# An output projection by seven products: four of them accumulate in one pair of banks, two operands are loaded in place, and part of the sums goes to GpSimd

## The chip, the cores and the metric

The kernel runs on one core of a Trainium2 chip. The time is that of the device in microseconds (us) for one execution. The engines of a core are TensorE (PE, matrix products; PEld is its loading of weights), VectorE (DVE), ScalarE (ACT), GpSimd (POOL) and SyncE (SP), which issues all DMA transfers of this kernel from one queue. Operands lie in SBUF, products in eight PSUM banks of 128 x 512 float32.

## The reference

One layer with four groups of mixers, each 512 wide, over 1024 tokens. Only the last line is touched by the change: the four mixers' outputs, side by side 1024 x 2048, are multiplied by a 2048 x 2048 matrix and added to x, all in float32.

```python
h = rms_norm(x, norm_g[l]) @ w_in[l]
...
y_a = gmlp_mixer(a_u, a_v, a_v_gain[l], a_ws[l], a_bs[l]) * jax.nn.silu(a_z)
y_b = dsa_mixer(...) * jax.nn.silu(b_z)
y_c = mla_mixer(...) * jax.nn.silu(c_z)
y_d = band_mixer(...) * jax.nn.silu(d_z)
x = x + jnp.concatenate([y_a, y_b, y_c, y_d], axis=-1) @ w_out[l]
```

## The kernel before

Most of the program computes the input projections and the four mixers; each mixer leaves its output y transposed (feature rows, token columns) in DRAM as `y_d`. The last input projection, that of A's gate, ends at about 1594 us, and the output projection takes the rest.

The output projection is done in two halves. The first takes groups B and D and adds them to x, with the result in DRAM (`pt_d`); the second takes groups C and A and adds them to that, with the result in `out`. Within a half the two token halves and the two groups form a 2 x 2 block matrix: a11 and a21 are the first group's first and last 512 tokens, a12 and a22 the second group's. The block product is made with seven products instead of eight (Strassen's method in Winograd's form): S1 to S4 are sums and differences of these blocks, and the weight blocks b are combined in the same way into t1 to t4. `prepare` makes the seven operands of a half: it loads y in tiles `ys` (128 x 1024, three buffers), forms the sums, and splits each operand into a high part `yh` (a cast on ACT) and a low part `yl` (a difference on DVE). A float32 product then takes three matmuls: high x high, high x low, low x high. The high and low parts of a half take seven of the eight large buffers that hold x and its low parts until the last input projection has read them, so each operand can be written only when a quarter of x has been read for the last time.

`out_unit` is called four times per half, for 512 output columns each; the text numbers the units 0 to 7. A unit loads four weight tiles `wo` and four residual tiles `xr` (one for each token half t and row pair jp, 128 x 2 x 512), combines the weights on DVE, splits them into `wh` (ACT) and `wl` (POOL) with three buffers each, runs the seven products and adds them to the residual tiles. A product is 48 matmuls (two halves of four 128-row steps, four blocks of rows) into two PSUM banks. Units 0 to 7 all use the same banks: X and Y from the four of `pp`, Z and W from the other four. DVE adds products from PSUM to `xr`; the product P1 is first copied to SBUF by ACT (`p1`), as three residual blocks need it.

The order on PE is written out by hand; that on the other engines is set by a scheduler when the program is built, in which the operands' and the weights' work has high priority and the adds to the residual have not. Each engine works through its queue in order. An instruction waits for the semaphores of what it reads and of what must have read its target before.

Of the kernel before, what the change touches and what calls it, by code (L numbers as in the profile page):

```python
# [18 lines left out]
P = 128  # L19
# [116 lines left out]
def build(tc, i, out, dbg=None):  # L136
# [1105 lines left out]
    A11, S2, S1, A12, S3, A22, S4 = range(7)  # L1242
# [6 lines left out]
    def load_y(g, kt):  # L1249
        t = op.tile([P, SEQ], F32, tag="ys", name="ys", bufs=3)  # L1250
        S.dma_start(t, y_d[512 * g + P * kt:512 * g + P * (kt + 1)])
        return t

    def prepare(g1, g2, part):
        for at in (S3, A22, S4) if part else (A11, S2, S1, A12):
            slots[at] = (big("th", "yh"), big("tl", "yl"))
        with hi_prio():
            if part == 0:
# [52 lines left out]
    def out_unit(g1, g2, c0, src, dst, rp, last):  # L1311
        cs = slice(c0, c0 + 512)
        ks1 = [load_wo(g1, h, c0) for h in range(2)]
        ks2 = [load_wo(g2, h, c0) for h in range(2)]
# [6 lines left out]
        with hi_prio():  # L1321
            ws["b11"] = [split_w(b11) for b11, _ in ks1]
# [5 lines left out]
            ws["t2"] = [split_w(t) for t in t2]  # L1328
            ws["t1"] = [split_w(b11) for b11, _ in ks1]
            ws["b21"] = [split_w(b21) for b21, _ in ks2]  # L1330
            for (_, b12), (_, b22) in zip(ks1, ks2):
                V.tensor_tensor(b12, b22, b12, op=ALU.subtract)
            ws["t3"] = [split_w(b12) for _, b12 in ks1]
            for (b21, _), t in zip(ks2, t2):
                V.tensor_tensor(b21, b21, t, op=ALU.subtract)
            ws["t4"] = [split_w(b21) for b21, _ in ks2]
            ws["b22"] = [split_w(b22) for _, b22 in ks2]
# [4 lines left out]
        def add(t, n, pss):  # L1342
            for jp in range(2):
                o = res[t, jp][:, :, 256 * n:256 * n + 256]
                V.tensor_tensor(o, o, f(pss[jp]), op=ALU.add)  # L1345
# [26 lines left out]
        for jp in range(2):  # L1372
            store(1, jp, 0, 2)
        if last:
            for jp in range(2):
                store(0, jp, 0, 1)
        add(0, 1, Z)
        for jp in range(2):
            store(0, jp, int(last), 2)

    for n, (g1, g2) in enumerate(((1, 3), (2, 0))):
        for part in range(2):
            prepare(g1, g2, part)
# [4 lines left out]
        for c in range(4):  # L1388
            out_unit(g1, g2, 512 * c, x_d if n == 0 else pt_d, pt_d if n == 0 else out, rp, n == 1 and c == 3)
# [35 lines left out]
```

## Time and profile before

| | |
|---|---|
| median of 3 runs | 1953.63 us (1952.82 to 1954.27) |
| the profiled execution | 1952.85 us |
| its span (what the trace covers) | 1951.0 us |
| PE, DVE, ACT, POOL busy | 97%, 61%, 40%, 37% |
| output projection, roughly | 1594 us to the end |

The time of the profiled execution is 1.85 us more than its span. A busy share of PE counts any time in which a matmul is under way; it does not say how fast the matmuls follow each other. The granted clock (PEclk) is a share of 2.4 GHz.

### The profile page before, as it was taken

How to read it: one execution, taken by the hardware profiler on the slowest of the kernel's cores; microseconds unless marked ns; L12 is line 12 of the kernel's file. 1: busy time of each engine (PE TensorE's matmuls, PEld its weight loads, DVE VectorE, ACT ScalarE, POOL GpSimd, SP SyncE). 2: the span in 40 equal slices, each digit the busy share in tenths (PEclk: the TensorE clock that was granted, in tenths of full speed). 3: DMA queues.
4: the chain of work that ended last, by engine and by line, in shares of the span. 5: the costliest groups of instructions: out<-in, count | busy, mean ns of one | idle time of the engine just before them, and what ended most of it. 6: DMA issues, size and time to landing. Idle time of an engine off the chain costs nothing.

```text
span 1951.0 us, 34949 instructions
## 1 busy us (share of the span) xinstructions
PE 1886.5 (97%) x13068; PEld 1755.6 (90%) x13068; DVE 1189.0 (61%) x3057; ACT 778.0 (40%) x1565; POOL 718.4 (37%) x784
## 2 busy tenths in 40 slices
PE   5999999999999999999999999999999998998999
PEld 4988998899888999999998889998888778998999
DVE  6514899887466553488836665734343568569644
ACT  6424533331455454344325555644453243223221
POOL 4121256763344443222223333422222133444543
PEclk8999999999999999999999999999999998999999
DMA  7231122223322222333334443243333756447443
GB/s 220 87 109 33 33 66 71 71 66 85 102 81 74 59 66 68 112 127 116 103 106 117 103 117 93 68 138 96 98 98 117 256 202 204 144 158 253 141 140 120
DMA packets 186269, 220.40 MB, mean 113 GB/s; under 512 B 26051, under 2 KB 136820, under 8 KB 185972
## 3 DMA queue, kind: packets, MB, share of 16 engines
q1 hardware_dynamic: 186100, 218.17, 37.0%
q8 instruction: 103, 1.69, 0.4%
q14 instruction: 66, 0.54, 0.1%
HBM read 153.35 MB, written 60.58 MB: 110 GB/s over the span
## 4 chain that ended last, share of the span: by engine, by line
PE 85%; DVE 6%; DMA 5%; SPq 1%; issue 1%; ACT 1%; POOL 1%; DVEq 0%; POOLq 0%; ACTq 0%
PE pp L206 60%; PE sc L206 14%; PE po L206 6%; PE sc L210 5%; DMA duo<-vd_d 1%; DMA ys<-y_d 1%; DMA nat<-qk_d 1%; DVE yl L243 1%; SPq L302 1%; DVE ys L1279 0%; DVE xr L1345 0%; DVE xr L1353 0%; DMA sw<-in_w_in 0%; DMA wr<-in_w_in 0%; SPq L327 0%
## 5 line engine op out<-in xcount | busy, mean ns | idle before, releaser
L420 POOL TENSOR_TENSOR wl<-wr,wh 128x512 fp32r<-128x512 f32 x192 | 255.1, 1329 | 526.4 <-ACT wh L419 470.1
L206 PE MATMUL pp<-wh,xh 128*128 128x256 f32 x1536 | 436.9, 284 | 0.0
L206 PE MATMUL pp<-wh,xl 128*128 128x256 f32 x1536 | 433.5, 282 | 0.0
L206 PE MATMUL pp<-wl,xh 128*128 128x256 f32 x1536 | 432.6, 282 | 0.0
L206 PE MATMUL pp<-xh,wh 128*128 128x512 f32 x768 | 309.2, 403 | 0.0
L206 PE MATMUL pp<-xh,wl 128*128 128x512 f32 x768 | 304.4, 396 | 0.0
L206 PE MATMUL pp<-xl,wh 128*128 128x512 f32 x768 | 304.0, 396 | 0.0
L206 PEld LDWEIGHTS pp<-wl,xh 128*128 128x128 f32 x1536 | 290.6, 189 | 1.2
L206 PEld LDWEIGHTS pp<-wh,xh 128*128 128x128 f32 x1536 | 289.8, 189 | 1.2
L206 PEld LDWEIGHTS pp<-wh,xl 128*128 128x128 f32 x1536 | 288.8, 188 | 0.0
L419 ACT CAST wh<-wr 128x512 fp32r<-128x512 f32 x192 | 118.9, 619 | 358.0 <-PE pp L206 312.9
L1292 POOL TENSOR_TENSOR wl<-wo,wh 128x512 fp32r<-128x512 f32 x96 | 138.9, 1451 | 169.4 <-ACT wh L1291 153.0
L530 POOL TENSOR_SCALAR sS<-sS,den 128x640 f32<-128x640 f32 (+7 forms) x160 | 115.9, 726 | 215.8 <-DVE den L529 156.8
L206 PEld LDWEIGHTS pp<-xh,wl 128*128 128x128 f32 x768 | 144.5, 188 | 35.0
L206 PEld LDWEIGHTS pp<-xl,wh 128*128 128x128 f32 x768 | 145.0, 189 | 28.9
L206 PEld LDWEIGHTS pp<-xh,wh 128*128 128x128 f32 x768 | 144.7, 188 | 29.2 <-issue 0.3
L528 ACT ACTIVATE sS<-sS,nm 128x640 f32<-128x640 f32 (+7 forms) x160 | 119.0, 744 | 125.3 <-DVE nm L525 111.9
L206 PE MATMUL pp<-wh,yh 128*128 128x256 f32 x512 | 147.3, 288 | 16.9 <-DVE xr L1345 13.9
L206 PE MATMUL pp<-wl,yh 128*128 128x256 f32 x512 | 146.4, 286 | 2.8 <-POOL wl L1292 2.7
L206 PE MATMUL pp<-wh,yl 128*128 128x256 f32 x512 | 146.0, 285 | 0.0
L700 DVE TENSOR_SCALAR_CACHE_REDUCE t<-score,cand 128x896 bf16<-128x896 f32 (+4 forms) x155 | 135.9, 877 | 4.2
L243 DVE TENSOR_TENSOR pl<-sc,ph 128x512 fp32r<-128x512 f32 (+1 forms) x152 | 92.2, 616 | 55.6 <-ACT ph L242 48.6
(262 smaller groups left out, 4115.2 us busy)
## 6 DMA issues: line engine op xcount, KB each, us to landing
wr<-in_w_in SPq DMA_DIRECT2D x192, 256.0 KB, 2.8
ys<-y_d SPq DMA_DIRECT2D x32, 512.0 KB, 3.8
wo<-in_w_out SPq DMA_DIRECT2D x32, 512.0 KB, 3.8
xt<-in_x SPq DMA_DIRECT2D x32, 256.0 KB, 4.7
xr<-in_x SPq DMA_DIRECT2D x16, 512.0 KB, 4.9
pt_d<-xr SPq DMA_DIRECT2D x16, 512.0 KB, 6.6
xr<-pt_d SPq DMA_DIRECT2D x16, 512.0 KB, 5.4
out<-xr SPq DMA_DIRECT2D x14, 512.0 KB, 6.9
```

Source lines behind the costliest of these rows:

```text
L206: T.matmul(o, l, r, start=start, stop=stop, skip_group_check=True)
L210: T.transpose(o, t, ident)
L243: V.tensor_tensor(lo, src, hi.bitcast(F32), op=ALU.subtract)
L302: S.dma_start(raw[:, :, o:o + n], rows[:, c0:c0 + n].rearrange("(k p) c -> p k c", p=P))
L419: A.copy(hi, raw)
L420: G.tensor_tensor(lo, raw, hi.bitcast(F32), op=ALU.subtract)
L528: A.activation(sS[:, :tot], sS[:, :tot], AF.Exp, bias=nm[:, 0:1], accum_out=den[:, 0:1])
L530: G.tensor_scalar(sS[:, :tot], sS[:, :tot], den[:, 1:2], 0.5, op0=ALU.mult, op1=ALU.mult)
L700: V.tensor_scalar(t1[:, :n], score[:, SOFF[b]:SOFF[b] + n], th, None, op0=op, op1=ALU.add, accum_out=cnt[:, b - 2:b - 1])
L1292: G.tensor_tensor(lo, src, hi.bitcast(F32), op=ALU.subtract)
```

## The change

Of the seven products, four (A11, S2, S3 and A22) now accumulate in one pair of banks, X. After each of the first three ACT copies what the bank holds (`keep`), and the copy is added to a residual block. The other three share Y. So a unit needs four banks; even units take those of `pp`, odd units the other four. The products come in another order (A11, A12, S2, S1, S3, S4, A22) and the weight combinations change their signs accordingly. Three of the adds of a copy are done by GpSimd instead of DVE.

In `prepare` the operands A11 and A12, which need no sums, are loaded straight into the tile of their low part and split there. The differences and sums for S3 and S4 move to GpSimd, with S3 kept in four tiles `s3` of its own. The weights of a half's first unit are loaded ahead of its operands.

```diff
-    A11, S2, S1, A12, S3, A22, S4 = range(7)
+    PRODUCTS = A11, A12, S2, S1, S3, S4, A22 = range(7)
...
-                for kt in range(4):
-                    q, r = load_y(g1, kt), load_y(g2, kt)
-                    a11, a21, a12, a22 = q[:, 0:512], q[:, 512:1024], r[:, 0:512], r[:, 512:1024]
-                    split_y(kt, A11, a11)
-                    V.tensor_tensor(a22, a21, a22, op=ALU.add)
-                    V.tensor_tensor(a11, a22, a11, op=ALU.subtract)
-                    split_y(kt, S2, a11)
-                    split_y(kt, S1, a22)
-                    split_y(kt, A12, a12)
-                return
-            for kt in range(4):
-                q = load_y(g1, kt)
-                V.tensor_tensor(q[:, 0:512], q[:, 0:512], q[:, 512:1024], op=ALU.subtract)
-                split_y(kt, S3, q[:, 0:512])
+            for at, k in ((A11, 0), (A12, 1)):
+                hi, lo = slots[at]
+                for kt in range(4):
+                    r0 = 512 * gs[k] + P * kt
+                    S.dma_start(lo[:, kt].bitcast(F32), y_d[r0:r0 + P, 0:512])
+                    split(hi[:, kt], lo[:, kt], lo[:, kt].bitcast(F32))
             for kt in range(4):
-                r = load_y(g2, kt)
-                a12, a22 = r[:, 0:512], r[:, 512:1024]
+                a11, a21 = load(0, kt)
+                a22 = load(1, kt)[1]
+                V.tensor_tensor(a22, a21, a22, op=ALU.add)
+                V.tensor_tensor(a11, a22, a11, op=ALU.subtract)
+                split_y(kt, S2, a11)
+                split_y(kt, S1, a22)
+            s3 = [op.tile([P, 512], F32, tag="s3", name="s3", bufs=4) for _ in range(4)]
+            for kt in range(4):
+                a11, a21 = load(0, kt)
+                G.tensor_tensor(s3[kt], a11, a21, op=ALU.subtract)
+                split_y(kt, S3, s3[kt])
+            for kt in range(4):
+                a12, a22 = load(1, kt)
+                G.tensor_tensor(a12, a12, a22, op=ALU.subtract)
+                G.tensor_tensor(a12, a12, s3[kt], op=ALU.add)
+                split_y(kt, S4, a12)
                 split_y(kt, A22, a22)
-                V.tensor_tensor(a12, a12, a22, op=ALU.subtract)
-                for t in slots[S3]:
-                    V.tensor_tensor(a12, a12, t[:, kt].bitcast(F32), op=ALU.add)
-                split_y(kt, S4, a12)
...
-        X, Y = ([pp.tile([P, 512], F32, tag="pp", name="pp", bufs=4) for _ in range(2)] for _ in range(2))
-        Z, W = [bank() for _ in range(2)], [bank(), obank()]
+        if odd:
+            X, Y = [bank() for _ in range(2)], [bank(), obank()]
+        else:
+            X, Y = ([pp.tile([P, 512], F32, tag="pp", name="pp", bufs=4) for _ in range(2)] for _ in range(2))
...
+        def keep(pss):
+            ts = [rp.tile([P, 512], F32, tag="p1", name="p1", bufs=6) for _ in range(2)]
+            for t, ps in zip(ts, pss):
+                with hi_prio():
+                    A.copy(t, ps)
+            return ts
...
-        product(X, A11, ws["b11"], True)
-        for jp in range(2):
-            p1 = rp.tile([P, 512], F32, tag="p1", name="p1", bufs=2)
-            A.copy(p1, X[jp])
-            for t, n in ((0, 1), (1, 1), (1, 0)):
-                o = res[t, jp][:, :, 256 * n:256 * n + 256]
-                V.tensor_tensor(o, o, f(p1), op=ALU.add)
-        product(Y, S2, ws["t2"], True)
+                eng.tensor_tensor(o, o, f(pss[jp]), op=ALU.add)
+
+        product(X, A11, ws[A11], True)
+        add(0, 0, keep(X), G)
+        product(Y, A12, ws[A12], True)
+        add(0, 0, Y)
+        product(X, S2, ws[S2], False)
+        add(0, 1, keep(X), G)
+        product(Y, S1, ws[S1], True)
+        z1 = keep(Y)
+        product(X, S3, ws[S3], False)
+        add(1, 1, keep(X), G)
+        add(1, 1, z1)
+        product(Y, S4, ws[S4], False)
         add(0, 1, Y)
-        product(Z, S1, ws["t1"], True)
-        add(1, 1, Z)
-        product(X, A12, ws["b21"], False)
-        add(0, 0, X)
-        product(Y, S3, ws["t3"], False)
-        add(1, 1, Y)
-        add(1, 0, Y)
-        product(W, A22, ws["t4"], True)
-        add(1, 0, W)
-        product(Z, S4, ws["b22"], False)
...
+        product(X, A22, ws[A22], False)
+        add(1, 0, X)
```

Two places in the engines' queues matter below, both in unit 0. The first is POOL's queue. Before, it holds the weights' low parts one after the other (here those of the second to fifth product, L1292):

```order
L1292 TENSOR_TENSOR wl_18528<-t2_18521,wh_18527 128x512
L1292 TENSOR_TENSOR wl_18532<-t2_18524,wh_18531 128x512
L1292 TENSOR_TENSOR wl_18536<-wo_18497,wh_18535 128x512
L1292 TENSOR_TENSOR wl_18540<-wo_18499,wh_18539 128x512
L1292 TENSOR_TENSOR wl_18544<-wo_18501,wh_18543 128x512
L1292 TENSOR_TENSOR wl_18548<-wo_18503,wh_18547 128x512
```

In the changed kernel the queue at the same place reads as follows. L1298 is a weight's low part (wl_18548 is the third product's second, wl_18552 and wl_18556 are the fourth product's), L1283 and L1284 make S4, and L1359 adds a kept product to a residual tile (xr_18513 and xr_18517 are the first token half's, p1_18639 and p1_18640 the first product).

```order
L1298 TENSOR_TENSOR wl_18548<-t2_18540,wh_18547 128x512
L1283 TENSOR_TENSOR ys_18492<-ys_18492 128x512
L1284 TENSOR_TENSOR ys_18484<-ys_18484,s3_18453 128x512
L1359 TENSOR_TENSOR xr_18513<-xr_18513,p1_18639 128x2x256
L1284 TENSOR_TENSOR ys_18492<-ys_18492,s3_18454 128x512
L1298 TENSOR_TENSOR wl_18552<-wo_18366,wh_18551 128x512
L1298 TENSOR_TENSOR wl_18556<-wo_18368,wh_18555 128x512
L1283 TENSOR_TENSOR ys_18500<-ys_18500 128x512
L1359 TENSOR_TENSOR xr_18513<-xr_18513,p1_18743 128x2x256
L1298 TENSOR_TENSOR wl_18564<-wo_18366,wh_18563 128x512
L1359 TENSOR_TENSOR xr_18517<-xr_18517,p1_18640 128x2x256
```

So operand work and adds to the residual now stand between the weights' low parts, and the first product's add to the second residual tile comes last of these rows.

The second place is DVE's queue around its first add of a product from PSUM. Before (L1345 adds from PSUM, L1353 adds the copied product, L1279 and L243 are operand work, L1335 weights):

```order
L1353 TENSOR_TENSOR xr_18505<-xr_18505,p1_18635 128x2x256
L1335 TENSOR_TENSOR wo_18501<-wo_18501,t2_18521 128x2x256
L1279 TENSOR_TENSOR ys_18474<-ys_18474,yh_18430 128x512
L1353 TENSOR_TENSOR xr_18507<-xr_18507,p1_18635 128x2x256 x2
L1335 TENSOR_TENSOR wo_18503<-wo_18503,t2_18524 128x2x256
L243 TENSOR_TENSOR yl_18435<-ys_18465,yh_18434 128x512
L1345 TENSOR_TENSOR xr_18505<-xr_18505,pp_18581 128x2x256
```

In the changed kernel (L1359 adds from PSUM here, pp_18589 and pp_18590 being the pair Y; yl_18385 and yl_18387 are S4's and A22's low parts, yl_20338 is already that of the second half's A11):

```order
L243 TENSOR_TENSOR yl_18385<-ys_18476,yh_18384 128x512
L243 TENSOR_TENSOR yl_18387<-ys_18476,yh_18386 128x512
L243 TENSOR_TENSOR yl_18387<-ys_18484,yh_18386 128x512
L243 TENSOR_TENSOR yl_18387<-ys_18492,yh_18386 128x512
L243 TENSOR_TENSOR yl_20338<-yl_20338,yh_20337 128x512
L243 TENSOR_TENSOR yl_18385<-ys_18484,yh_18384 128x512
L243 TENSOR_TENSOR yl_20338<-yl_20338,yh_20337 128x512
L1359 TENSOR_TENSOR xr_18513<-xr_18513,pp_18589 128x2x256
L243 TENSOR_TENSOR yl_20338<-yl_20338,yh_20337 128x512 x2
L243 TENSOR_TENSOR yl_18385<-ys_18492,yh_18384 128x512
L243 TENSOR_TENSOR yl_18387<-ys_18500,yh_18386 128x512
L1359 TENSOR_TENSOR xr_18517<-xr_18517,pp_18590 128x2x256
```

The adds of the copied product have left this queue; the two adds from PSUM stand between differences of operands that POOL has made before, and each reads a residual tile to which POOL adds first.

## Rows read from the trace of the kernel before

**Rows 1.** The page: the span, and busy time of each engine.

```profile
span 1951.0 us, 34949 instructions
...
PE 1886.5 (97%) x13068; PEld 1755.6 (90%) x13068; DVE 1189.0 (61%) x3057; ACT 778.0 (40%) x1565; POOL 718.4 (37%) x784
```

**Rows 2.** Waits of PE from 1580 us on: total, times, longest, in us.

```profile
PE pp L206 <- DVE xr L1345: 13.9, 3, 5.4
PE pp L206 <- POOL wl L1292: 2.7, 3, 1.5
PE sc L206 <- POOL wl L1292: 2.6, 4, 1.0
```

**Rows 3.** Busy us by stretch: PE, PEld, DVE, ACT, POOL, clock, DMA share, GB/s.

```profile
1594.00:1631.00 37.00, 25.78 (x200) 24.70 (x199) 34.65 (x46) 13.38 (x23) 17.00 (x9) 0.90 0.63 217
1689.40:1729.70 40.30, 40.30 (x338) 40.30 (x337) 22.44 (x29) 9.76 (x16) 19.21 (x14) 1.00 0.47 158
```

**Rows 4.** The chain that ended last, from 1500 us: start, length, what.

```profile
1630.85 6.74 PE pp L206 x42
...
1643.35 5.76 PE sc L206 x48
1649.11 11.52 PE pp L206 x96
...
1729.75 8.65 PE pp L206 x72
...
1807.02 7.31 PE pp L206 x42
...
1825.86 11.52 PE pp L206 x96
```

**Rows 5.** PE in order of time: last input projection, first stall on DVE's add.

```profile
1593.80 0.40 PE L206 MATMUL pp<-xh,wl 128*128 128x512 f32 x1
...
1625.54 0.55 PE L206 MATMUL pp<-wh,yh 128*128 128x256 f32 x1 [4.82 <-DVE xr L1345]
```

**Rows 6.** DVE's groups from 1594 us on, by form: adds from PSUM, from SBUF.

```profile
L1345 DVE TENSOR_TENSOR xr<-xr,pp 128x512 f32<-128x512 f32 x64 | 41.8, 682 | 37.1 <-PE pp L206 37.1
L1353 DVE TENSOR_TENSOR xr<-xr,p 128x512 f32<-128x512 f32 x48 | 40.8, 879 | 39.1 <-DMA xr<-pt_d 13.7 <-DMA xr<-in_x 12.1 <-ACT p L1350 11.1
```

**Rows 7.** DVE in order of time, 1786 to 1792 us.

```profile
1786.77 1.29 DVE L243 TENSOR_TENSOR yl<-ys,yh 128x512 fp32r<-128x512 f32 x2
1787.98 1.77 DVE L1279 TENSOR_TENSOR ys<-ys,yh 128x512 f32<-128x512 f32 x1
1789.79 1.67 DVE L1279 TENSOR_TENSOR ys<-ys,yl 128x512 f32<-128x512 f32 x1
```

**Rows 8.** POOL in order of time: two beside adds from PSUM, two beside rows 7.

```profile
1643.39 2.56 POOL L1292 TENSOR_TENSOR wl<-wo,wh 128x512 fp32r<-128x512 f32 x2 [3.56 <-DMA wo<-in_w_out]
...
1787.86 3.05 POOL L1292 TENSOR_TENSOR wl<-wo,wh 128x512 fp32r<-128x512 f32 x2 [2.33 <-ACT wh L1291]
```

**Rows 9.** ACT in order of time: casts that waited for x's second quarter.

```profile
1571.04 1.14 ACT L242 CAST yh<-ys 128x512 fp32r<-128x512 f32 x2 [2.70 <-PE pp L206]
```

**Rows 10.** ACT's groups from 1594 us on, by form.

```profile
L242 ACT CAST yh<-ys 128x512 fp32r<-128x512 f32 x39 | 23.7, 619 | 67.1 <-DVE ys L1279 24.1 <-DMA ys<-y_d 18.2 <-DVE ys L1271 14.1
...
L1350 ACT COPY p<-pp 128x512 f32<-128x512 f32 x16 | 9.2, 583 | 4.8 <-PE pp L206 4.6
```

**Rows 11.** DMA issues from 1594 us on: count, size, median us to landing.

```profile
ys<-y_d SPq DMA_DIRECT2D x20, 512.0 KB, 3.7
...
pt_d<-xr SPq DMA_DIRECT2D x16, 512.0 KB, 6.6
...
y_d<-hs SPq DMA_DIRECT2D x4, 256.0 KB, 4.8
```

**Rows 12.** DVE in unit 5: the first use of its third residual tile.

```profile
1837.04 0.69 DVE L1353 TENSOR_TENSOR xr<-xr,p 128x512 f32<-128x512 f32 x1 [2.19 <-issue]
```

More of the change, by code (lines that the diff above doesn't have):

```diff
@@ L1247, in split_y, with renew, prepare, load @@
         split(*(t[:, kt] for t in slots[at]), src)
[L1249 to L1255, printed above, removed]
-            slots[at] = (big("th", "yh"), big("tl", "yl"))
+    def renew(ats):
+        for at in ats:
+            slots[at] = (big("th", "yh"), big("tl", "yl"))
+    def prepare(gs):
+        renew(PRODUCTS)
+        def load(k, kt):
+            t = op.tile([P, SEQ], F32, tag="ys", name="ys", bufs=3)
+            S.dma_start(t, y_d[512 * gs[k] + P * kt:512 * gs[k] + P * (kt + 1)])
+            return t[:, 0:512], t[:, 512:1024]
@@ L1309, in rows_of, with out_unit @@
         return slice(512 * t + 256 * jp, 512 * t + 256 * jp + 256)
-    def out_unit(g1, g2, c0, src, dst, rp, last):
+    def out_unit(ks, c0, src, dst, rp, odd, last):
         cs = slice(c0, c0 + 512)
-        ks1 = [load_wo(g1, h, c0) for h in range(2)]
-        ks2 = [load_wo(g2, h, c0) for h in range(2)]
+        ks1, ks2 = ks
         res = {}
@@ L1321, in out_unit @@
         with hi_prio():
-            ws["b11"] = [split_w(b11) for b11, _ in ks1]
+            ws[A11] = [split_w(b11) for b11, _ in ks1]
+            ws[A12] = [split_w(b21) for b21, _ in ks2]
             t2 = []
@@ L1327, in out_unit @@
                 V.tensor_tensor(t2[-1], b22, b11, op=ALU.subtract)
-            ws["t2"] = [split_w(t) for t in t2]
-            ws["t1"] = [split_w(b11) for b11, _ in ks1]
-            ws["b21"] = [split_w(b21) for b21, _ in ks2]
+            ws[S2] = [split_w(t) for t in t2]
+            ws[S1] = [split_w(b11) for b11, _ in ks1]
             for (_, b12), (_, b22) in zip(ks1, ks2):
                 V.tensor_tensor(b12, b22, b12, op=ALU.subtract)
-            ws["t3"] = [split_w(b12) for _, b12 in ks1]
@@ L1334, in out_unit @@
             for (b21, _), t in zip(ks2, t2):
                 V.tensor_tensor(b21, b21, t, op=ALU.subtract)
-            ws["t4"] = [split_w(b21) for b21, _ in ks2]
-            ws["b22"] = [split_w(b22) for _, b22 in ks2]
-        X, Y = ([pp.tile([P, 512], F32, tag="pp", name="pp", bufs=4) for _ in range(2)] for _ in range(2))
-        Z, W = [bank() for _ in range(2)], [bank(), obank()]
-        f = lambda t: t.rearrange("p (j c) -> p j c", j=2)
-        def add(t, n, pss):
+            ws[S3] = [split_w(b12) for _, b12 in ks1]
@@ new lines, in out_unit @@
+            ws[S4] = [split_w(b22) for _, b22 in ks2]
+            ws[A22] = [split_w(b21) for b21, _ in ks2]
+        if odd:
+            X, Y = [bank() for _ in range(2)], [bank(), obank()]
+        else:
+            X, Y = ([pp.tile([P, 512], F32, tag="pp", name="pp", bufs=4) for _ in range(2)] for _ in range(2))
+        f = lambda t: t.rearrange("p (j c) -> p j c", j=2)
+        def keep(pss):
[4 more added lines that the diff above has]
+            return ts
@@ L1343, in add @@
+        def add(t, n, pss, eng=V):
             for jp in range(2):
                 o = res[t, jp][:, :, 256 * n:256 * n + 256]
-                V.tensor_tensor(o, o, f(pss[jp]), op=ALU.add)
-        product(X, A11, ws["b11"], True)
-        for jp in range(2):
-            p1 = rp.tile([P, 512], F32, tag="p1", name="p1", bufs=2)
-            A.copy(p1, X[jp])
-            for t, n in ((0, 1), (1, 1), (1, 0)):
-                o = res[t, jp][:, :, 256 * n:256 * n + 256]
-                V.tensor_tensor(o, o, f(p1), op=ALU.add)
@@ L1372, in out_unit @@
         for jp in range(2):
-            store(1, jp, 0, 2)
+            store(0, jp, 0, 2)
         if last:
             for jp in range(2):
-                store(0, jp, 0, 1)
-        add(0, 1, Z)
+                store(1, jp, 1, 2)
+        product(X, A22, ws[A22], False)
+        add(1, 0, X)
         for jp in range(2):
-            store(0, jp, int(last), 2)
+            store(1, jp, 0, 1 if last else 2)
     for n, (g1, g2) in enumerate(((1, 3), (2, 0))):
-        for part in range(2):
-            prepare(g1, g2, part)
+        load_ks = lambda c: [[load_wo(g, h, 512 * c) for h in range(2)] for g in (g1, g2)]
+        ks = load_ks(0)
+        prepare((g1, g2))
         if n == 0:
@@ L1388, in build @@
         for c in range(4):
-            out_unit(g1, g2, 512 * c, x_d if n == 0 else pt_d, pt_d if n == 0 else out, rp, n == 1 and c == 3)
+            out_unit(ks if c == 0 else load_ks(c), 512 * c, x_d if n == 0 else pt_d, pt_d if n == 0 else out, rp, c % 2, n == 1 and c == 3)
     if dbg is not None:
```

1 line of the change is left out of this document (removed).

## The prediction

> **What bounds the kernel now.** The page comes first: TensorE (PE) is busy for 97% of the span [rows 1], so a stage can gain only what PE stands idle there. The table by stages shows where that is. In a middle unit of the output projection PE is busy for all of 40.3 us, with VectorE (DVE) at 22.4 and GpSimd (POOL) at 19.2 us. From 1594 to 1631 PE works for 25.8 of 37 us, DVE for 34.7 [rows 3]. The chain gives the unit boundaries [rows 4]. A product is 48 matmuls in 5.76 us, so a unit of seven needs 40.32 us. Unit 0 runs from 1594.20, where the last input projection ends [rows 5], to 1649.11: 54.9 us, 14.6 too many. Units 3 and 4 together run from 1729.75 to 1825.86: 96.1 us instead of 80.6, 15.5 too many. The other units show no excess, so some 30 us are at stake, all where the operands of a half are being made. The table of waits names the releaser of the largest stalls: DVE's add of a product into the residual, 13.9 us [rows 2]. It stands in DVE's queue behind the sums and differences of the operands, and PE must not write that bank before it is read [rows 5].
>
> The second thing to see is why DVE is slow there. Its adds from PSUM take 682 ns whatever happens, its adds between SBUF tiles 879 ns on average [rows 6]. The timeline shows the cause: two such operations start every 0.60 us when alone, but take 1.77 and 1.67 us when two POOL operations run beside them, and those two take 3.05 us together instead of the 2.56 beside adds from PSUM [rows 7, 8]. So the SBUF operations of DVE and those of POOL exclude each other for most of their length: one of each costs 1.72 us (the mean of the two DVE rows), against 1.28 for POOL alone and 0.60 for DVE alone.
>
> **What the change does, part by part.** *Residual adds.* A unit loses 12 of its 20 DVE adds: four of the six between SBUF tiles, and eight from PSUM, which did not exclude POOL. POOL gains six, of the size of its own 1.28 us rows. In SBUF time that DVE and POOL must share, a unit goes from (6 + 8) x 0.60 + 14 x 1.28 = 26.3 us to (2 + 8) x 0.60 + 20 x 1.28 = 31.6 us. The eight are DVE's operations on weights. That fits in 40.3, so in units 1, 2, 5, 6 and 7 I cost it at nothing: a weight part has two half products, 5.76 us, between its buffer's release and its use, and the cast (0.62) and POOL's difference (1.28) take 1.9 of them. Without that cover two POOL adds in front of a part would cost up to 2.6 us.
>
> *Copies.* ScalarE makes eight copies of a product per unit instead of two, 6 x 0.58 = 3.5 us [rows 10], beside 9.8 us of work in 40.3 [rows 3]. PE may not go on in the bank until its copy is done, but always has another product of 5.76 us in between, so nothing is added. Unit 0's first copy is an exception: its tile lies where the last gate results are still being stored, and those stores land 4.8 us after issue [rows 11]; the third product would wait for it until about 1613, which is earlier than the wait found below.
>
> *Operands.* Per half DVE goes from 52 operations to 36, all between SBUF tiles, and POOL from none to 12: 52 x 0.60 = 31.2 us of shared time become 36 x 0.60 + 12 x 1.28 = 37.0. The two loaded in place need no sums, and eight loads of 256 KB more, 2 MB. I cost the transfer at nothing, since DMA is at a share of 0.63 there [rows 3]; at that window's 217 GB/s it would be 9.7 us of one queue, none of it ahead of the first product.
>
> *Where the stall goes.* In unit 0 the fourth product writes the bank pair of the second. So it waits for DVE's two adds of the second product, and the second of these waits for POOL's add of the first product on the same residual tile. In POOL's new order this add is the nineteenth operation, counted from the second of its four differences for the operand S3 (ten are operand work, six weight parts, three residual adds), and ahead of DVE's add stand 19 operations between SBUF tiles from there.
>
> When do the nineteen begin? The buffers of the third and fourth operand come free with the second quarter of the last projection, at 1571.0 [rows 9]. The first pair is read out at 1572.9 (two casts, two differences). Three load buffers then make a ring: 3.7 us landing [rows 11], two sums, a cast, two differences, 3.0 us. Two more rounds, with 1.8 us for three weight operations that the new order puts between, lead to 1588.1, and the last load of this group lands at 1591.8. POOL's first difference for S3 reads the load behind it, ends near 1595 because DVE is running without a gap, and its buffer's next load lands at about 1599; I take 1600.0 as the start, with 1598 and 1601.5 as bounds. PE's restart takes what it took before, 6.74 us for the 42 matmuls left, at a lower granted clock (0.90 in rows 3), then three products. So unit 0 ends at 1600.0 + 19 x 1.72 + 0.7 (DVE's add) + 6.74 + 17.28 = 1657.4, against 1649.11: 8.3 us later.
>
> Units 3 and 4 go the same way. Counted from unit 3's start, its weight part for the seventh product cannot be written before ten half products are done, 28.8 us, and two POOL adds stand ahead of it; with these POOL reaches the operand work at about 34. From there 22 POOL operations lead to the add that unit 4's fourth product waits for, with 20 of DVE beside them: 34 + 20 x 1.72 + 2 x 1.28 + 0.7 + 7.31 (the restart row of this half) + 17.28 = 96.25 us, against 96.11. So here it is even: the stalls on DVE that go and the queue on POOL that comes weigh the same.
>
> The sum is 8.3 + 0.1 = 8.4 us on the profiled execution's 1952.85, 1961.25. The median of the runs is 0.8 above that execution, which gives **1962.0 us**.
>
> The price that decides is that of a POOL operation in these two queues, 41 of them. Alone it is 1.28, with one DVE operation for each it is 1.72. I take 1.72 because the counts are nearly equal (19 to 19, 20 to 22) and both queues are in order. Each 0.1 us moves the end by 4.1 us; the forecast's mean is 1.70, no change lies at 1.49.
>
> The Trainium skill (SBUF — State Buffer, "SBUF: two separate sides") says that a VectorE operation with two SBUF inputs and a GpSimd operation take the shared port pair as an exclusive lock for the whole instruction, so that the loser waits for all of it. The trace agrees in kind, not quite in size: by it a pair would cost 1.28 + 0.60 = 1.88 us, where the rows show 1.72. This rule speaks against the change, which moves work from one side of that lock to the dearer other side.
>
> **The rivals.** *POOL keeps ahead (faster).* If DVE's operations fall into gaps that POOL leaves anyway, where it waits for a load or a cast, a POOL operation costs 1.28. Then unit 0 ends at 1600.0 + 24.3 + 0.7 + 24.02 = 1649.0, and units 3 and 4 take 34 + 28.2 + 0.7 + 24.6 = 87.5 us: together 8.7 us less, 1944.9. For it: the new DVE queue is shorter and often waits. Against it: both queues hold one for one what the other must wait for. It is faster by over 0.2% below 1.40 us.
>
> *Half of it (no change).* Between 1.40 and 1.59 us the result stays within 3.9 us of 1953.63, the 0.2% that a measurement of this kernel can tell from no change.
>
> *The whole lock.* At 1.88 us for a pair unit 0 ends at 1660.4 and units 3 and 4 take 99.5 us: +14.7, so 1968.3.
>
> *A late residual load.* In unit 5 of before the third residual tile is used 11.2 us after the unit's start [rows 4, 12]. POOL now needs that tile for its second add, and the weight part behind it is due at 14.4. With 1.28 for each the part is ready at 13.8, so 0.6 us are left. If stores of a unit's end (6.6 us [rows 11]) land 2 us later than now, each of units 5 to 7 loses 1.4 us: 4.2 on top, 1966.
>
> **How the numbers follow.** My forecast, a pace from 1.59 to 1.8, gets 0.37; the whole lock 0.11; the late load 0.06; no change 0.21; POOL ahead 0.25. So slower 0.54, same 0.21, faster 0.25. The range takes in the bounds of the pace, from 1944 (POOL alone) to 1973 (the whole lock and the late load, 1972.5).
>
> **What the profile afterwards would show.** Right: PE's longest waits are in unit 0's and unit 4's third and fourth products, on POOL's weight parts and on DVE's add from PSUM, which itself waits for POOL; POOL's mean is over 1.5 us there; PE restarts the fourth product near 1633 and unit 1 begins near 1657; middle units stay at 40.3 us. Wrong: the fourth product restarts before 1627, or POOL stands idle between 1600 and 1630, or waits for casts and loads rather than for DVE. Wrong in another way: PE stalls in units 5 to 7 on a weight part.

## The result, and the profile after

The changed kernel takes 1975.03 us (median of 4 runs, 1968.83 to 1975.93), beside 1953.95 for the kernel before in the same session. The ratio is 1.0096, 95% interval 1.0068 to 1.0123: slower by 13 to 24 us, where 8.4 were forecast; the median lies 2 us above the upper end of the range. The profiled execution took 1975.93 us.

The page, beside [rows 1]: PE's share is a point lower, POOL has 100 us more, DVE 58 us less.

```profile
span 1974.2 us, 34987 instructions
...
PE 1896.3 (96%) x13068; PEld 1764.3 (89%) x13068; DVE 1131.1 (57%) x2929; ACT 803.2 (41%) x1613; POOL 818.8 (41%) x856
```

PE's waits from 1580 us on, beside [rows 2]. In all they are 35.4 us; all five rows of that view of before were 22.2.

```profile
PE pp L206 <- DVE xr L1359: 17.5, 3, 8.0
PE pp L206 <- POOL wl L1298: 6.7, 8, 1.9
PE sc L206 <- POOL wl L1298: 3.8, 5, 1.0
PE pp L206 <- DVE hs L1223: 3.2, 1, 3.2
PE pp L206 <- ACT p L1353: 2.8, 1, 2.8
PE sc L206 <- ACT wh L1297: 1.4, 1, 1.4
```

Busy us by stretch (columns as in [rows 3]): units 0, 3 and 4, first before, then changed. The matmuls of a unit without stalls take 40.3 us at a granted clock of 1.00; in the changed kernel they take 46.2, 43.1 and 45.3 in these units, at mean clocks of 0.86, 0.96 and 0.91.

```profile
1595.30:1648.95 53.65, 43.53 (x337) 42.65 (x337) 46.32 (x62) 16.41 (x28) 23.27 (x14) 0.90 0.57 191
...
1729.59:1773.90 44.31, 41.44 (x339) 40.59 (x338) 35.90 (x45) 16.93 (x30) 19.58 (x13) 1.00 0.57 186
1773.90:1825.69 51.79, 43.63 (x338) 42.60 (x337) 46.90 (x61) 16.01 (x28) 24.95 (x15) 0.93 0.62 216
```

```profile
1597.60:1659.40 61.80, 46.20 (x338) 45.31 (x337) 47.22 (x41) 22.27 (x40) 50.27 (x32) 0.86 0.59 199
...
1741.10:1788.60 47.50, 43.10 (x339) 42.08 (x337) 26.61 (x31) 19.23 (x35) 27.14 (x20) 0.96 0.59 201
1788.60:1846.70 58.10, 45.29 (x338) 43.84 (x337) 36.47 (x34) 18.59 (x33) 49.67 (x33) 0.91 0.54 189
```

The stalls of PE on which the rest turns, in order of time: two in unit 0, two in unit 3, one in unit 4. The first matmul after four of them takes 0.55 to 0.58 us instead of 0.28.

```profile
1628.92 0.55 PE L206 MATMUL pp<-wh,yh 128*128 128x256 f32 x1 [4.54 <-DVE xr L1359]
...
1635.52 0.58 PE L206 MATMUL pp<-wh,yh 128*128 128x256 f32 x1 [4.98 <-DVE xr L1359]
...
1757.07 0.38 PE L206 MATMUL sc<-wh,yh 128*128 128x256 f32 x1 [1.39 <-ACT wh L1297]
1758.42 0.58 PE L206 MATMUL sc<-wl,yh 128*128 128x256 f32 x1 [0.97 <-POOL wl L1298]
...
1822.57 0.58 PE L206 MATMUL pp<-wh,yh 128*128 128x256 f32 x1 [8.00 <-DVE xr L1359]
```

Unit 0 on POOL, then on DVE. From 1602.14 to 1634.3 POOL makes nineteen operations, with 0.3 us of idle time between them; the last is its second add of the first product (the first of the two at 1632.62). DVE's add behind it ends, and PE restarts at 1635.52.

```profile
1609.01 1.74 POOL L1283 TENSOR_TENSOR ys<-ys 128x512 f32<-128x512 f32 x1
...
1620.85 1.73 POOL L1359 TENSOR_TENSOR xr<-xr,p 128x512 f32<-128x512 f32 x1
...
1632.62 3.38 POOL L1359 TENSOR_TENSOR xr<-xr,p 128x512 f32<-128x512 f32 x2
```

```profile
1616.29 6.84 DVE L243 TENSOR_TENSOR yl<-ys,yh 128x512 fp32r<-128x512 f32 x4
1623.06 1.78 DVE L243 TENSOR_TENSOR yl<-yl,yh 128x512 fp32r<-128x512 f32 x1
...
1628.70 2.83 DVE L243 TENSOR_TENSOR yl<-yl,yh 128x512 fp32r<-128x512 f32 x2
...
1634.79 0.68 DVE L1359 TENSOR_TENSOR xr<-xr,pp 128x512 f32<-128x512 f32 x1
```

The rows `yl<-yl,yh` were not foreseen: they are operands of the second half, loaded in place into the one buffer that is free, and made in the middle of unit 0.

Unit 3: SP, ACT and POOL in order of time. SP issues the in-place loads at 1748.96. ACT stands 7.69 us at the cast of such an operand, with the weight cast of 1756.40 behind it. POOL's second add waits 5.49 us for its residual tile, with a weight part behind it at 1757.10. Later in the unit the same pattern returns: a weight part at 1776.83 waits for its cast, which stands in ACT's queue behind an operand cast of 1774.88.

```profile
1748.50 0.37 SPq L1324 DMA_DIRECT2D xr<-in_x  x1
1748.96 1.85 SPq L1267 DMA_DIRECT2D yl<-y_d  x4
```

```profile
1755.88 0.62 ACT L242 CAST yh<-yl 128x512 fp32r<-128x512 f32 x1 [7.69 <-DMA yl<-y_d]
1756.40 0.61 ACT L1297 CAST wh<-t 128x512 fp32r<-128x512 f32 x1
...
1774.88 1.35 ACT L242 CAST yh<-ys 128x512 fp32r<-128x512 f32 x2 [3.60 <-DVE ys L1272]
1776.14 0.61 ACT L1297 CAST wh<-wo 128x512 fp32r<-128x512 f32 x1
```

```profile
1755.31 1.27 POOL L1359 TENSOR_TENSOR xr<-xr,p 128x512 f32<-128x512 f32 x1 [5.49 <-DMA xr<-in_x]
1757.10 1.27 POOL L1298 TENSOR_TENSOR wl<-t,wh 128x512 fp32r<-128x512 f32 x1 [0.52 <-ACT wh L1297]
...
1776.83 1.27 POOL L1298 TENSOR_TENSOR wl<-wo,wh 128x512 fp32r<-128x512 f32 x1 [4.17 <-ACT wh L1297]
...
1782.37 1.59 POOL L1279 TENSOR_TENSOR s<-ys 128x512 f32<-128x512 f32 x1
...
1788.04 1.70 POOL L1298 TENSOR_TENSOR wl<-wo,wh 128x512 fp32r<-128x512 f32 x1 [2.38 <-ACT wh L1297]
1790.51 1.83 POOL L1279 TENSOR_TENSOR s<-ys 128x512 f32<-128x512 f32 x1 [0.77 <-DMA ys<-y_d]
```

Where the time went, by PE's own rows (starts of the 48 matmuls of each product). "Ahead" is from the start of the last input projection's matmul [rows 5] to the first output product; unit 0 runs from that product to unit 1's start; the last column runs to the last product's last matmul; all is the sum. All in us.

| kernel | ratio to before (95% interval) | ahead | unit 0 | units 1, 2 | units 3, 4 | units 5 to 7 | all |
|---|---|---|---|---|---|---|---|
| before | | 1.5 | 53.7 | 80.6 | 96.1 | 120.8 | 352.7 |
| changed | 1.0096 (1.0068 to 1.0123) | 0.2 | 61.8 | 81.7 | 105.6 | 123.2 | 372.6 |
| e1 | 1.0076 (1.0058 to 1.0093) | 0.2 | 62.6 | 80.6 | 103.9 | 120.8 | 368.2 |
| e2 | 1.0041 (1.0026 to 1.0055) | 0.2 | 53.4 | 83.2 | 104.6 | 122.6 | 363.9 |
| e3 | 1.0019 (1.0007 to 1.0032) | 0.2 | 54.7 | 80.6 | 102.2 | 120.8 | 358.6 |
| e4 | 1.0078 (1.0063 to 1.0093) | 0.2 | 62.7 | 82.7 | 101.8 | 121.6 | 369.0 |
| e5 | 1.0076 (1.0052 to 1.0101) | 3.6 | 57.0 | 82.9 | 101.6 | 125.8 | 370.9 |
| e6 | 0.9978 (0.9963 to 0.9993) | 1.6 | 49.7 | 80.6 | 96.4 | 120.8 | 349.1 |
| e7 | 0.9999 (0.9988 to 1.0010) | 2.2 | 54.4 | 80.6 | 96.1 | 120.8 | 354.1 |
| e8 | 1.0014 (0.9998 to 1.0030) | 1.6 | 56.0 | 80.8 | 96.4 | 121.4 | 356.2 |
| e9 | 1.0058 (1.0039 to 1.0076) | 0.2 | 56.5 | 82.8 | 101.0 | 123.4 | 363.9 |
| e10 | 0.9920 (0.9893 to 0.9947) | 1.6 | 50.3 | 80.6 | 87.2 | 120.8 | 340.5 |
| e11 | 1.0055 (1.0033 to 1.0077) | 3.2 | 53.7 | 83.5 | 96.0 | 125.1 | 361.4 |
| e12 | 0.9999 (0.9986 to 1.0012) | 1.8 | 50.6 | 82.6 | 92.1 | 121.9 | 349.0 |

The change costs 19.9 us here. The profiled executions differ by 23.1; the other 3 us lie ahead of this stage, and in the fourteen executions of the table the last input projection's matmul started anywhere from 1591.9 to 1600.6 us (1593.8 in before, 1597.3 in the changed kernel, 1592.7 in e10). So this table tells kernels apart better than single times do. Still, each of its rows is one execution: "all" less that of before and the same difference by the ratio lie up to 3.5 us apart (e12: -3.7 and -0.2), so a few microseconds between two rows are no result by themselves. PE's busy time over the eight units is 337.2 us against 330.3 before: of the 19.9 some 7 are matmuls that take longer after stalls, 6.0 of them in units 0, 3 and 4, where the granted clock is lower, and 13.2 (35.4 less 22.2) are the waits themselves.

### The profile page after: what moved, and what is told of

Its sections match the earlier page's. It is cut to its first block, busy times and chain, and to the rows that moved or that the text cites. A ratio compares the mean times of both kernels' runs of the same rounds, so it can differ in the third digit from the quotient of the medians.

```text
span 1974.2 us, 34987 instructions
## 1 busy us (share of the span) xinstructions
PE 1896.3 (96%) x13068; PEld 1764.3 (89%) x13068; DVE 1131.1 (57%) x2929; ACT 803.2 (41%) x1613; POOL 818.8 (41%) x856
## 3 DMA queue, kind: packets, MB, share of 16 engines
q8 instruction: 103, 1.69, 0.3%
## 4 chain that ended last, share of the span: by engine, by line
PE 76%; DMA 11%; DVE 5%; POOL 4%; issue 2%; SPq 1%; ACT 1%; POOLq 0%; DVEq 0%; ACTq 0%
PE pp L206 54%; PE sc L206 11%; PE po L206 5%; PE sc L210 5%; POOL wl L1298 2%; DMA pt_d<-xr 2%; DMA ys<-y_d 1%; DMA wo<-in_w_out 1%; POOL xr L1359 1%; DVE yl L243 1%; DMA nat<-qk_d 1%; DMA duo<-vd_d 1%; DMA yl<-y_d 1%; DMA wr<-in_w_in 1%; DMA out<-xr 1%
## 5 line engine op out<-in xcount | busy, mean ns | idle before, releaser
L1298 POOL TENSOR_TENSOR wl<-wo,wh 128x512 fp32r<-128x512 f32 x96 | 137.0, 1430 | 82.0 <-ACT wh L1297 78.4
L206 PE MATMUL pp<-wh,yh 128*128 128x256 f32 x448 | 130.9, 292 | 23.6 <-DVE xr L1359 17.5
L206 PE MATMUL pp<-wl,yh 128*128 128x256 f32 x448 | 130.7, 292 | 6.7 <-POOL wl L1298 6.7
L206 PE MATMUL pp<-wh,yl 128*128 128x256 f32 x448 | 129.9, 290 | 0.0
L243 DVE TENSOR_TENSOR pl<-sc,ph 128x512 fp32r<-128x512 f32 (+1 forms) x152 | 92.2, 616 | 56.2 <-ACT ph L242 49.3
```

The source lines that it names most:

```text
L206: T.matmul(o, l, r, start=start, stop=stop, skip_group_check=True)
L243: V.tensor_tensor(lo, src, hi.bitcast(F32), op=ALU.subtract)
L1298: G.tensor_tensor(lo, src, hi.bitcast(F32), op=ALU.subtract)
```

## The experiments

The expectations count from the first output product to the last, so without "ahead". Each experiment changes the changed kernel, except e7. Medians of "before" beside them were 1953.9 to 1954.9.

**e1: residual adds back on DVE.**

```diff
-        add(0, 0, keep(X), G)
+        add(0, 0, keep(X))
...
-        add(0, 1, keep(X), G)
+        add(0, 1, keep(X))
...
-        add(1, 1, keep(X), G)
+        add(1, 1, keep(X))
```

> One part undone: the three residual adds of kept products go back from GpSimd to VectorE; the operand sums stay on GpSimd. My theory (GpSimd's in-order queue, where each operation beside a VectorE operation takes 1.7 us instead of 1.3, is what TensorE waits for, and GpSimd's residual adds, held by the late third residual load, hold the weight parts behind them): in units 2, 3, 5 and 6 the third-product stalls (1.0, 4.3, 1.0 and 1.4 us) go or shrink, since VectorE waits for the residual tile and GpSimd goes on with weight parts; units 0 and 4 lose two to four GpSimd operations ahead of the fourth product's operand, about 1.7 us each, and gain as many VectorE ones of 0.7 us: about 2 us each. Together 6 to 10 us below the changed kernel's 1975.0, so 1965 to 1969. Rival (GpSimd's adds are hidden and the time comes from the accumulation in one bank pair, its copies and the in-place loads): within 2 us of 1975.

Measured: 1970.23 us. The third-product stalls of units 2, 5 and 6 are gone, that of unit 3 fell from 4.3 to 0.9. But unit 0 is no shorter (62.6): of 4.4 us gained 3.5 lie in units 1, 2 and 5 to 7, less in all than expected. My reason for unit 0, a residual add standing in POOL's queue, is not needed: with the add on DVE it stands behind DVE's low parts, which go at POOL's pace (four in 6.85 us from 1614.87).

**e2: operand sums for S3 and S4 back on DVE.**

```diff
-                G.tensor_tensor(s3[kt], a11, a21, op=ALU.subtract)
+                V.tensor_tensor(s3[kt], a11, a21, op=ALU.subtract)
...
-                G.tensor_tensor(a12, a12, a22, op=ALU.subtract)
-                G.tensor_tensor(a12, a12, s3[kt], op=ALU.add)
+                V.tensor_tensor(a12, a12, a22, op=ALU.subtract)
+                V.tensor_tensor(a12, a12, s3[kt], op=ALU.add)
```

> The other part undone: the operand sums for S3 and S4 (twelve operations in each of the two stages) go back from GpSimd to VectorE; GpSimd keeps the residual adds. My theory: in unit 0 GpSimd has some nine operations instead of nineteen between 1602 and the restart, VectorE some ten more; the sum of the two engines' time falls from 19 x 1.7 to about 9 x 1.7 plus 10 x 0.9 plus what VectorE does alone, so unit 0 is 3 to 7 us shorter than 61.8, units 3 and 4 together as much; the third-product stalls of units 2, 5 and 6 stay. Together 6 to 12 us below 1975.0, so 1963 to 1969. Rival (the bank order and in-place loads): within 2 us of 1975. A second rival (VectorE is the bound in these stages, as in the kernel before with 13.9 us of waits on its residual adds): no gain, or 3 us slower.

Measured: 1963.38 us. Unit 0 is 8.4 us shorter and back at the time of before with the sums alone undone. Units 3 and 4 give back only 1.0. So the total lies in the expected range, but neither part does (3 to 7 us each).

**e3: both, the edits of e1 and e2 together.**

> Both parts undone: residual adds of kept products and operand sums on VectorE; what is left of the change is the accumulation of four products in one bank pair with the copies between, the in-place loads and the new order of products. My theory: the GpSimd part of the loss goes, 12 to 16 us, so 1959 to 1963; what stays is the late third residual load in units 5 and 6 as a VectorE wait that TensorE does not see, and the in-place loads in unit 3. Rival (bank order, copies and in-place loads carry the loss): 1970 to 1976.

Measured: 1958.56 us, just below the expected range, and 14.0 us less in the table. POOL's share is gone from the middle units, but units 3 and 4 still lose 6.1 us. In unit 3 ACT still stands at an in-place operand, with a weight cast behind it; ACT in order of time:

```profile
1749.70 0.62 ACT L242 CAST yh<-yl 128x512 fp32r<-128x512 f32 x1 [6.50 <-DMA yl<-y_d]
1750.23 0.61 ACT L1297 CAST wh<-t 128x512 fp32r<-128x512 f32 x1
```

**e4: residual tiles loaded in the order of their use.**

```diff
-        for jp in range(2):
-            for t in range(2):
+        for t in range(2):
+            for jp in range(2):
```

> Nothing moved between engines: the four residual tiles of a unit are allocated and loaded in the order in which the new product order wants them, both tiles of the first token half ahead of those of the second. My theory: the first product's second add no longer waits for a load that stands third, so the stalls of units 2, 5 and 6 (1.0, 1.0 and 1.4 us) go and unit 3 may lose part of its 4.3 us: 3.4 to 6 us below 1975.0, so 1969 to 1971.6. Rival (these stalls come from GpSimd's pace, not from the load): within 1 us of 1975.

Measured: 1969.91 us, 3.6 less in the table: the expected size, partly in other places. Units 5 to 7 gain 1.6, units 3 and 4 gain 3.8; units 1 and 2 are 0.9 longer, and unit 2 keeps a stall of 1.15 us on a weight part behind POOL's second add, which waits 2.98 us there; the trace names PE and no longer the load as what it waits for. So the late load is one cause of these stalls; what holds the add in unit 2 is not shown. Nor does the new order always bring the load in time, as e11 shows below.

**e5: A11 and A12 cast from the `ys` tiles instead of loaded in place.**

```diff
-            for at, k in ((A11, 0), (A12, 1)):
-                hi, lo = slots[at]
-                for kt in range(4):
-                    r0 = 512 * gs[k] + P * kt
-                    S.dma_start(lo[:, kt].bitcast(F32), y_d[r0:r0 + P, 0:512])
-                    split(hi[:, kt], lo[:, kt], lo[:, kt].bitcast(F32))
             for kt in range(4):
                 a11, a21 = load(0, kt)
-                a22 = load(1, kt)[1]
+                a12, a22 = load(1, kt)
+                split_y(kt, A11, a11)
+                split_y(kt, A12, a12)
```

> Nothing moved between engines: the operands A11 and A12 no longer go by their own loads into the place of their low parts, but are cast from the same ys tiles that the sums for S2 and S1 use, as in the kernel before; eight transfers a stage fewer. Measured on the trace from the first output product to the last: before 351.2 us, changed 372.4. My theory (in the second stage ScalarE's queue stands 7.7 us at the cast of an in-place operand whose load waits behind stores, and the weight casts behind it are late): unit 3 loses the 4.3 us at its third product, GpSimd reaches the operand sums earlier and unit 4 gives back 2 to 4; unit 0 unchanged. The stretch 364 to 369, the whole 4 to 8 us below the changed kernel. Rival (GpSimd's second residual add, which waits for its load, is what holds the weight parts in unit 3 as in units 2, 5 and 6): within 2 us of the changed kernel.

Measured: 1969.83 us, and 367.3 without "ahead": both in the expected ranges, but not by the expected parts. Units 3 and 4 gain 3.9. Unit 0, expected unchanged, gains 4.8, but 3.4 come back as a wait ahead of it and 3.7 in the middle units, where residual loads are later (POOL's second add in unit 1 waits 5.06 us for one). In all the profiled execution shows 1.7 us, the ratios some 4, and the size stays open.

**e6: e3 and e5 together.** What is left of the change is the order of products in one bank pair, with its copies, and the early load of a half's first weights, which no experiment undoes.

> Everything that went to GpSimd is back on VectorE and the operands A11 and A12 come from the ys tiles: of the change only the product order with four products in one bank pair and its copies is left. The stretch from the first output product to the last: before 351.2 us, with the in-place loads 358.4. My theory (what is left of the loss is the in-place loads and the queues that they hold up): 351 to 354, the whole within 2 us of the kernel before. Rival (the order of products in one bank pair costs by itself, as the fourth product now wants an operand that comes last): 356 to 359.

Measured: 1950.40 us, faster than before, and 347.5 without "ahead", below both ranges. So the rival falls, and my theory was too high by 3.5 us: what is left costs nothing, it gains 3.6 us in the table and some 4 by the ratio. The in-place loads cost 9.5 (358.6 less 349.1), 5.0 in unit 0 less the 1.3 that come back ahead of it, and 5.8 in units 3 and 4.

**e7: the kernel before, with its sums on GpSimd.**

```diff
-                V.tensor_tensor(q[:, 0:512], q[:, 0:512], q[:, 512:1024], op=ALU.subtract)
+                G.tensor_tensor(q[:, 0:512], q[:, 0:512], q[:, 512:1024], op=ALU.subtract)
...
-                V.tensor_tensor(a12, a12, a22, op=ALU.subtract)
-                for t in slots[S3]:
-                    V.tensor_tensor(a12, a12, t[:, kt].bitcast(F32), op=ALU.add)
+                G.tensor_tensor(a12, a12, a22, op=ALU.subtract)
+                for eng, t in zip((V, G), slots[S3]):
+                    eng.tensor_tensor(a12, a12, t[:, kt].bitcast(F32), op=ALU.add)
```

> The kernel before with one part of the change alone: twelve of its sixteen operand sums for S3 and S4 in each of the two stages go from VectorE to GpSimd. My theory (GpSimd's queue at 1.7 us an operation beside VectorE is what costs, in any product order): unit 0 6 to 9 us longer than its 53.7, units 3 and 4 together 1 to 6 longer than their 96.1; the stretch 358 to 366 against 351.2, the whole 7 to 15 us above the kernel before. Rival (the sums cost only in the new product order, whose fourth product wants them first): within 2 us of the kernel before, or faster, as VectorE, for which TensorE waits 13.9 us there, has twelve operations fewer.

Measured: 1955.42 us, no change. My theory's 7 to 15 us fell, and the rival was right. PE's waits show a swap: on DVE's adds 3.6 us instead of 13.9, on POOL's weight parts 13.3 instead of the 5.3 of [rows 2].

```profile
PE pp L206 <- POOL wl L1292: 9.4, 5, 3.3
...
PE sc L206 <- POOL wl L1292: 3.9, 7, 1.0
PE pp L206 <- DVE xr L1345: 3.6, 2, 3.1
```

**e8: residual adds on GpSimd, all else mended: the edits of e2, e4 and e5.**

> Of the change the bank order, the copies and the residual adds on GpSimd stay; the operand sums are on VectorE, A11 and A12 come from the ys tiles, and the residual tiles are loaded in the order in which they are wanted. My theory: unit 0 as with the sums alone undone (53.4), units 1, 2, 5 and 6 at 40.3 to 40.9, units 3 and 4 at the kernel before's 96.1 or a little under, since GpSimd takes the adds that VectorE did: the stretch 348 to 353 against 351.2, so 1951 to 1956 beside 1954. Rival (GpSimd's adds hold the weight parts in units 3 and 4 whatever the loads do): 355 to 360, so 1958 to 1963.

Measured: 1958.74 us, at the rival's lower end in time and just below it in the table (354.6 without "ahead"). PE waits 4.8 us for an operand's high part and 4.5 for a copy, both on ACT. In ACT's queue the copy stands behind an operand cast that waited 2.60 us for a sum of DVE, and the high part is such a cast, which waited 2.31 us for one.

**e9: a third bank pair.** S1 and S4 accumulate in two banks of the other parity, so the fourth product no longer overwrites the second's.

```diff
+            Z = [pp.tile([P, 512], F32, tag="pp", name="pp", bufs=4) for _ in range(2)]
         else:
...
+            Z = [bank() for _ in range(2)]
...
-        product(Y, S1, ws[S1], True)
-        z1 = keep(Y)
+        product(Z, S1, ws[S1], True)
+        z1 = keep(Z)
...
-        product(Y, S4, ws[S4], False)
-        add(0, 1, Y)
+        product(Z, S4, ws[S4], False)
+        add(0, 1, Z)
```

> The changed kernel with one thing more: S1 and S4 accumulate in a third bank pair Z instead of Y, so that the fourth product no longer writes over the bank whose sum the third-last residual add has still to read; GpSimd's work, the in-place loads and the order of products stay. The stretch from the first output product to the last: before 351.2 us, changed 372.4. Theory as it stands after the runs so far (GpSimd's late queue costs only because with two bank pairs the fourth product must wait for a VectorE add that stands behind GpSimd's first residual add): the stalls of 4.98 us in unit 0 and 8.0 in unit 4 go or come back shorter one or two products later; 358 to 366. Rival (TensorE would wait for the operands of S3 and S4 themselves, which come out of the same GpSimd queue): 369 to 373, with the stall renamed after an operand's part.

Measured: 1965.07 us, 8.7 less in the table, and 363.7 without "ahead", as my theory had it. The 17.5 us of waits on DVE's adds are gone altogether, those on weight parts rise from 10.5 to 22.3:

```profile
PE pp L206 <- POOL wl L1298: 15.3, 11, 4.4
PE sc L206 <- POOL wl L1298: 7.0, 7, 1.5
```

**e10: e6 with the third bank pair of e9.**

> All sums and adds on VectorE and A11 and A12 from the ys tiles (347.5 us from the first output product to the last, beside 351.2 before), and the third bank pair for S1 and S4. Theory: the one long stall left there, 8.8 us ahead of the fourth product of unit 4, goes or shrinks: 338 to 345, so about 1941 to 1948, faster than both kernels. Rival (the operands of S3 are no earlier than that stall's end, as the same VectorE queue makes them): 346 to 348.

Measured: 1937.42 us, ratio 0.9920: faster than both kernels, by 10 to 21 us against before, and 338.9 without "ahead", as expected. The 8.8 us stall of e6's unit 4 does not come back elsewhere; these are all of PE's waits from 1580 us on:

```profile
PE pp L206 <- ACT p L1351: 4.5, 1, 4.5
PE pp L206 <- POOL wl L1294: 3.4, 4, 1.5
PE pp L206 <- DVE hs L1223: 3.1, 2, 1.9
PE sc L206 <- POOL wl L1294: 0.9, 1, 0.9
```

**e11: GpSimd's whole share kept, the rest mended: the edits of e4, e5 and e9.**

> The changed kernel with GpSimd's whole share kept (operand sums and residual adds), and the three things around it mended: A11 and A12 from the ys tiles, residual tiles loaded in the order in which they are wanted, a third bank pair for S1 and S4. Theory (GpSimd's late queue costs only through what waits in order behind it: bank, weight parts, loads): 345 to 353 us from the first output product to the last, beside 351.2 before and 372.4 changed. Rival (GpSimd's pace of 1.7 us an operation beside VectorE is itself the bound of units 0 and 4): 358 to 366.

Measured: 1964.96 us, and 358.2 without "ahead"; the rival's range was right. The banks no longer hold anything, and still 20.9 us more (26 by the ratios) go by than in e10, which differs in POOL's share and in the order of the residual loads. PE waits 19.7 us for weight parts. Not all of it is POOL's pace, which the rival named: 7.1 of the 20.9 us lie in the middle units, and in unit 5 POOL's second add still waits 3.81 us for its residual load. In unit 0 DVE and POOL go in step from 1611 to 1626 us; DVE's rows come first, then POOL's:

```profile
1616.51 10.26 DVE L243 TENSOR_TENSOR yl<-ys,yh 128x512 fp32r<-128x512 f32 x6
```

```profile
1617.70 1.74 POOL L1280 TENSOR_TENSOR ys<-ys,s 128x512 f32<-128x512 f32 x1
1619.47 1.68 POOL L1357 TENSOR_TENSOR xr<-xr,p 128x512 f32<-128x512 f32 x1
1621.11 1.73 POOL L1294 TENSOR_TENSOR wl<-wo,wh 128x512 fp32r<-128x512 f32 x1
...
1843.02 1.26 POOL L1357 TENSOR_TENSOR xr<-xr,p 128x512 f32<-128x512 f32 x1 [3.81 <-DMA xr<-pt_d]
```

**e12: e8 with the third bank pair, so GpSimd has the residual adds alone.**

> Operand sums on VectorE, the three residual adds a unit on GpSimd, A11 and A12 from the ys tiles, residual tiles in the order wanted, and the third bank pair. Theory: as the same kernel with two pairs (354.6 us from the first output product to the last) less its bank waits (1.6 us named so, and the 11 us between third and fourth product in unit 4): 344 to 350. Rival (ScalarE's casts of operands and copies, 4.8 and 4.5 us there, are what remains): 353 to 355.

Measured: 1953.93 us and 347.2 without "ahead", as expected. Between e10 and e12 lie the residual adds (with the load order), 8.5 us; between e12 and e11 the sums, 12.4. By the ratios the two are some 15 and 11, so the first is known to several us only.

## Why the prediction was right in direction and too small

Undone one after another, the parts of the change add up to its 19.9 us. The differences are taken from the table; beside them stand those of the ratios, times 1954 us:

| step | all, us | cost | by the ratios |
|---|---|---|---|
| before to e6: order of products, one bank pair, copies, early weights | 352.7 to 349.1 | -3.6 | -4.3 |
| e6 to e3: in-place loads | 349.1 to 358.6 | +9.5 | +8.0 |
| e3 to e2: residual adds on GpSimd | 358.6 to 363.9 | +5.3 | +4.3 |
| e2 to changed: operand sums on GpSimd | 363.9 to 372.6 | +8.7 | +10.7 |

The shares depend on the order in which the parts are undone, as e5 shows.

**The pair price: right.** 1.72 us was taken; nineteen operations in unit 0 took 32.2 us, 1.69 each, with most rows at 1.71 to 1.75. In units 3 and 4 it was 1.62, since DVE there waited for casts now and then. Both rivals of a smaller price fall, and so does the whole lock at 1.88. The Trainium skill's rule (SBUF — State Buffer, "SBUF: two separate sides") holds in kind, as six DVE operations took 10.26 us beside POOL in e11; in size the trace stays under it.

**Unit 0: right.** 8.3 us were forecast from the end of the input projections; unit 0 with what lies ahead is 6.9 us longer (62.1 against 55.2). The restart came at 1635.5, after an input projection that ended 3.5 us later than before; the forecast said 1633. The path that I named, through POOL's residual add, is only one of two of equal length (e1); the sums make both (e2). That the size came out is in part luck: with what lies ahead, the new order gains 3.9 us in unit 0 (e6) and the in-place loads cost 3.7 (e3), neither of them a term of my sum, and the two cancel. The copies, costed at nothing, show no loss here, but not for my reason: the third product waited 2.83 us for one, which stood in ACT's queue behind casts that waited 2.30 us for POOL's sum; the fourth product's wait ended later.

**Units 3 and 4: the step that failed.** "With these POOL reaches the operand work at about 34": it reached it at 1782.37, 41.2 us after unit 3's start, and then stood idle for 3.6 us that the sum did not have. So +9.5 us came in the place of +0.1. Of the 7.2 us by which the start is late, 4.3 are unit 3's third product. The rest was not in my sum either: the weight part at 1776.83, ahead of two adds and the last part before 1782.37, waited 4.17 us for its cast, behind an operand cast that waited for a sum. The late third product is the doing of two things costed at nothing. One is the in-place loads: I priced their bytes and their distance from the first product, not the queues that they stand in. They leave SP 7.8 us into unit 3, behind three residual loads and the stores between them, and ACT's queue stands at the first cast of them, which begins 6.9 us after that. e6 against e3 shows it: without them units 3 and 4 are 5.8 us shorter. The other is the residual load, next. The two hang together: e1, e4 and e5 each undo one thing, and each leaves 0.9 to 1.4 of the 4.3 us.

**Middle units at nothing: wrong by 3.5 us.** The late residual load was a rival with 0.06; units 5 and 6 lose 1.0 and 1.4 us by it, unit 7 nothing, units 1 and 2 another 1.1. These are the stalls on a weight part that the prediction's last sign of being wrong names. e1 takes all of this away; e4 takes 1.6 of the 2.4 us in units 5 to 7 and adds 0.9 in units 1 and 2. I had a condition for it, stores 2 us later; the stores are later (7.5 us to landing instead of the 6.6 of [rows 11]), and the slack was 0.6.

**What was not weighed apart: the new order by itself.** It takes six of twenty adds a unit and four operations a half away. In e6 that gains 3.6 us, and in e10 with a third bank pair 12.2. So DVE's adds, PE's longest waits before (13.9 us), are no longer waited for in e10, and GpSimd's share relieves an engine that needs no relief; in the old order it trades one wait for another (e7). The Trainium skill (Perfetto Trace Analysis, "Matmuls") says that independent groups of matmuls should rotate through different PSUM banks so that reading one out lies beside the next. e9 and e10 agree, with 8.7 and 8.6 us for a third pair in the table, 7 and 11 by the ratios.

**Left open:** how much the in-place loads cost with GpSimd's share in place (e5), what the early weight loads do by themselves, and what else than its load holds POOL's second add in e4.

## What to carry to other kernels

When work is to move from VectorE to GpSimd, count the SBUF operations of both engines in each stage and price a pair by rows in which they run side by side; then ask whether the engine relieved will still be waited for after the rest of the change. A load into a buffer that comes free late can cost by its place in the queues, however few its bytes: find what is queued behind it on the engine that issues it and on the engine that first reads it. Give a product that starts afresh its own banks wherever the adds that free them lie in a busy queue.

## What was not expected of the hardware

A third of the loss, 7 of 19.9 us, is not waiting: after the stalls of unit 0's and unit 4's fourth products (4.5 to 8.0 us) matmuls take 0.55 to 0.58 us instead of 0.28 at first, and the mean granted clock of unit 0 is 0.86 (between the levels of 2.4 and 1.2 GHz) where it was 0.90. The trace of before had shown this with its 6.74 and 7.31 us restart rows [rows 4]; that each new stall brings it again was not in my sum.
